# A 2-layer RG-LRU and HGRN2 step: the low parts of weight blocks made by an accumulating DMA onto a negated rounded block instead of a GpSimd subtraction

## The chip, the cores and the metric

The kernel runs on one core of one Trainium2 chip. A core has TensorE (PE in the profile: matrix products; PEld is its weight load), VectorE (DVE), ScalarE (ACT), GpSimd (POOL) and SyncE (SP), each with its own in-order instruction queue, and 16 DMA engines that move data between HBM and the on-chip memory SBUF. Products are collected in PSUM banks. The metric is the device time of one execution in microseconds, the median over runs.

## The reference

One inference step of a trunk with two layers, D = 1024, on 1024 prompt positions and on 8 sequences of 4 sampled positions (1056 columns in all). Layer 0 is an RG-LRU block, layer 1 is HGRN2 with 8 heads of 128; each is `x + y @ w_out`.

```python
def _lru_layer(x, g_norm, w_in, conv_w, conv_b, w_r, b_r, w_i, b_i, lam, w_out, h0, buf):
    xn = _rmsnorm(x, g_norm)
    u = xn @ w_in                                   # 1024 -> 2 * 1536
    xb, gate = u[..., :W_LRU], u[..., W_LRU:]
    xc, new_buf = _causal_conv(xb, conv_w, conv_b, buf)
    h, h_last = _rg_lru(xc, w_r, b_r, w_i, b_i, lam, h0)
    y = (h * jax.nn.silu(gate.astype(jnp.float32))).astype(x.dtype)
    return x + y @ w_out, h_last.astype(x.dtype), new_buf.astype(x.dtype)

def _hgrn_layer(x, g_norm, w_in, lb, o_gain, w_out, S0):
    xn = _rmsnorm(x, g_norm)
    u = (xn @ w_in).astype(jnp.float32)             # 1024 -> 4 * 1024
    q, f, iv, gate = jnp.split(u, 4, axis=-1)
    ...
    o, S_T = _hgrn2_chunked(q, k, v, log_g, S0)
    o = o * lax.rsqrt(jnp.mean(o * o, axis=-1, keepdims=True) + EPS) * o_gain.reshape(H_B, DV_B).astype(jnp.float32)
    y = (o.reshape(Bsz, T, INNER_B) * jax.nn.silu(gate)).astype(x.dtype)
    return x + y @ w_out, S_T.astype(x.dtype)
```

All data is float32.

## The kernel before

**Three products for one.** Each float32 operand is split into a high part, which is the operand rounded to the matmul's format fp32r, and a low part, which is what the rounding left over. A product is three matmuls (`mm3`, L242 to L244): high by high, high weight by low data, low weight by high data. So every weight block needs a `hi` and a `lo` tile before it can be used.

**Weights.** `weights()` (L365) loads a weight in blocks of 512 columns (128 x 512 floats are 256 KB; the output projection of layer 0 has blocks of 384, that of layer 1 has 512 + 128). For each block a DMA on SP's queue fills one of three raw buffers (`wraw`, L309), ScalarE rounds it into one of four `whi` buffers (L377), and `subtract` (L322) writes raw minus `whi` into one of four `wlo` buffers. The engine is the parameter `e`, GpSimd unless told otherwise; only four of the six weights at the very start use VectorE. Two of these weights at the start, numbers 3 and 5, are written into longer-lived tiles `yh` and `yl`, and the first two weights of the last projection into tiles called `t`. The raw buffer can be loaded again once both the rounding and the subtraction have read it; a `whi` or `wlo` buffer can be written again once the last matmul that used it is over.

**Where it is used.** Layer 0: gate and convolution projections (`project0`: one weight of two blocks, then three chunks of 352 columns with 8 x 3 matmuls each; `by_chunk` with two weights taken in turn), and the output projections `out`. Layer 1: the first two weights (`first1`), the two weights that follow them (`ahead`, L920) and the four weights of head 1. The last two weights of head 1 are taken in turn for the last chunks. Heads 2 to 7 use `seven` (L1398), a scheme of seven products for eight; its `split` (L1423) has a subtraction of its own on GpSimd, on the same line L322. The last projection (L1616) uses `weights()` again. The data's high and low parts `t` for `seven` come from VectorE, ScalarE and GpSimd (`t<-R,t` and `t<-tmp,t` on L322).

**Around the products.** While PE multiplies, the recurrence of the head before is worked out by short stages (`burst1` to `burst4`), with doubling multiplies on VectorE (L1033, L1042), small products on PE (L1051, L1105, L1136) and predicated copies (L1055). L1496 combines the products of `seven` on VectorE.

**What sets the order.** Nothing is issued where it stands in the code. A planner (`Flow`) records each operation with its engine, a cost, the tiles that it reads and writes and a priority; it then lays a list schedule forward and backward eight times, keeps the best, and issues the operations in that order. For layer 0 it also tries 3000 random changes within the first 60 us of its plan. In the plan a GpSimd operation over n columns costs 0.1 + 0.00245 n us, an ACT one 0.25 + 0.0007 n, a DMA's issue 0.45 plus a lag that grows with its size:

```python
        def dma(dst, src, r=(), w=(), prio=5, kb=180, q=Q):
            fl.add("SP" if q is Q else "ACT", 0.45, lambda: q.dma_start(dst, src), r, w, prio, kb * (1.0 if r else 0.75))
...
        return self.HOP + b[6] + (2.15 + a[5] / 250.0 if a[5] else 0.0)
```

A VectorE operation marked `both` is planned longer when GpSimd is busy. So a change of one operation's engine or cost can move others. At the start PE also gets 48 matmuls on a tile of ones (`warm`, L727), at the lowest priority.

Of the kernel before, what the change touches and what calls it, by code (L numbers as in the profile page):

```python
# [14 lines left out]
F32 = mybir.dt.float32  # L15
# [3 lines left out]
AF = mybir.ActivationFunctionType  # L19
ALU = mybir.AluOpType  # L20
# [190 lines left out]
def tile_trunk(ctx: ExitStack, tc: tile.TileContext, xT, prm, hc, w0, wg, wo0, w1, wo1, s_in,  # L211
               yT, h_out, c_out, sp_out, ss_out):
    nc = tc.nc
    V, S, G, T, Q = nc.vector, nc.scalar, nc.gpsimd, nc.tensor, nc.sync
# [80 lines left out]
    with ExitStack() as l0:  # L295
        pl = l0.enter_context(tc.tile_pool(name="l0", bufs=1, reuse_waits="tile"))
        fl = Flow("PE")
# [10 lines left out]
        def dma(dst, src, r=(), w=(), prio=5, kb=180, q=Q):  # L308
            fl.add("SP" if q is Q else "ACT", 0.45, lambda: q.dma_start(dst, src), r, w, prio, kb * (1.0 if r else 0.75))  # L309

        def act(n, emit, r, w, prio=5, more=0.0):
            fl.add("ACT", 0.25 + 0.0007 * n + more, emit, r, w, prio)

        def dve(n, emit, r, w, prio=5, both=False):
            fl.add("DVE", 0.13 + 0.0011 * n, emit, r, w, prio, both=both)

        def pool(n, emit, r, w, prio=5):
            fl.add("POOL", 0.1 + 0.00245 * n, emit, r, w, prio)

        def subtract(e, n, b, x, a, r, w, prio):  # L320

            emit = lambda: e.tensor_tensor(b, x, a.bitcast(F32), op=ALU.subtract)  # L322
            if e is G:
                pool(n, emit, r, w, prio)
            else:
                dve(n, emit, r, w, prio, True)
# [38 lines left out]
        def weights(src, n, prio=2, e=G, at=None, q=Q, own=()):  # L365

            own = iter(own)
            got = []
            for a in range(0, n, 512):
                m = min(512, n - a)  # L370
                raw, *rk = next(own, None) or next(raws)
                if at:
                    (hi, hk), (lo, lk) = ((o[:, a:a + m], k) for o, k in at)
                else:
                    (hi, hk), (lo, lk) = next(his), next(los)
                dma(raw[:, :m], src[:, a:a + m], (), rk, prio, m / 2, q)
                act(m, lambda hi=hi, raw=raw, m=m: S.copy(hi[:, :m], raw[:, :m]), rk, (hk,), prio)  # L377
                subtract(e, m, lo[:, :m], raw[:, :m], hi[:, :m], (*rk, hk), (lk,), prio)
                got.append((hi, lo, hk, lk))

            def get(k):
                q = slice((k % 4) * 128, (k % 4 + 1) * 128)
                hi, lo, hk, lk = got[k // 4]
                return hi[:, q], lo[:, q], (hk, lk)

            return get
# [18 lines left out]
        def project0(items):  # L405

            for src, evac in items:
                w = weights(src, 1024)
                for c in range(NCH):
                    evac(c, *product(w, xcols(c)))  # L410
                    yield

        def by_chunk(items):

            ws = [weights(src, 1024) for src, _ in items]
            for c in range(NCH):
                for w, (_, evac) in zip(ws, items):
                    evac(c, *product(w, xcols(c)))
                    yield


        def squares(k, x, xk, acc, eng=None, own=None, mult=False):

            a, ak = acc
            sq, sk = next(own or ts) if k else acc
            if mult:
                pool(CH, lambda: G.tensor_tensor(sq[:, :CH], x, x, op=ALU.mult), (xk,), (sk,), 2)
            else:
                act(CH, lambda: S.activation(sq[:, :CH], x, AF.Square), (xk,), (sk,), 2)
            if k:  # L430
                e = eng or G
                (pool if e is G else dve)(CH, lambda: e.tensor_tensor(a[:, :CH], a[:, :CH], sq, op=ALU.add), (sk, ak), (ak,), 2)
# [22 lines left out]
        def scaled_parts(c, k, x, xk, bc, bk, g, gk, e, prio=1):  # L455
            a, b = xh[k][:, chunk(c)], xl[k][:, chunk(c)]
            dve(CH, lambda: V.scalar_tensor_tensor(x, x, g, bc, op0=ALU.mult, op1=ALU.mult), (xk, bk, gk), (xk,), prio)
            act(CH, lambda: S.copy(a, x), (xk,), (("xh", k, c),), prio)
            subtract(e, CH, b, x, a, (xk, ("xh", k, c)), (("xl", k, c),), prio)
# [164 lines left out]
        def out(g, src, dst):  # L624

            own = cycle([next(xos) for _ in range(NXO)] + [next(ts) for _ in range(3)] + [(x[:, :CH], k) for x, k in (next(xbs) for _ in range(3))])
            for m in range(KD):
                w = weights(wo0[m][:, 384 * g:384 * g + 384], 384)
                for c in range(NCH):
                    ps, pk = product(w, ycols(c))  # L630
                    x, xk = next(own)
                    dma(x, src[m][:, chunk(c)], ((g, m, c),), (xk,), 3)
                    dve(CH, lambda x=x, ps=ps: V.tensor_tensor(x, ps[:, :CH], x, op=ALU.add), (pk, xk), (xk,), 0)
                    dma(dst[m][:, chunk(c)], x, (xk,), ((g + 1, m, c),), 3)
                    yield
# [207 lines left out]
        raw = (halves[1][:8], [slots[i] for i in (1, 4, 7, 2, 5, 8)] + [halves[1][8], free[8]], free[:8])  # L843
# [82 lines left out]
    with ExitStack() as l1:  # L926
        p1 = l1.enter_context(tc.tile_pool(name="l1", bufs=1, reuse_waits="tile"))
        fl = Flow(side=0.4)
# [704 lines left out]
        for m in range(KD):  # L1633
            row = (xh, xl)[m // 4][4 + m % 4]
            hi, lo, hk, lk = row[:, :nl], row[:, nl:2 * nl], ("late", m, 0), ("late", m, 1)
            for k in (hk, lk):
                inherit(k, [("x", p, m % 4, x) for p in (2, 3) for x in range(2)])
            raw, rk = next(raws)
# [60 lines left out]
        for a, n in OUT:  # L1699
# [4 lines left out]
            for m in range(KD):  # L1704
# [5 lines left out]
                hi, lo, wk = late[m]  # L1710
# [97 lines left out]
```

## Time and profile before

| | |
|---|---|
| time, 3 runs | 1086.44 us median (1086.31 to 1087.67) |
| span of the profiled execution | 1084.3 us |
| PE busy, share of the span | 1056.6 us, 97% |
| DVE / POOL / ACT busy | 885.3 / 602.3 / 549.2 us |
| bytes moved by DMA | 103.05 MB |

The profiled execution is one of the same program; its span runs from the first to the last instruction that the profiler saw, and its whole time is not given apart, so the runs' median stands 2.1 us above the span. In the profile's rows an instruction is written as engine, line, operation, output <- inputs, and the tile's size. The groups' `<-` in the last column names what ended the engine's idle time.

### The profile page before, as it was taken

To read this page: it belongs to the slowest core of one execution; us is meant where nothing else is said; L and a number is where in the kernel's file an instruction comes from. 1 tells how busy PE (TensorE), PEld (TensorE's weight loads), DVE (VectorE), ACT (ScalarE), POOL (GpSimd) and SP (SyncE) were. 2 spreads that over 40 slices of the span, in tenths; PEclk is the share of its full clock that TensorE was granted. 3 is DMA by queue.
4 is the path that set the end of the run, shared out by engine and by line. 5 is a ranking of instruction groups with operands and counts; after the bars stand their busy time and mean duration, and the time that the engine had idled before them with its cause. 6 is when DMAs were issued, how large, how long until landed. Compare 5 with 4: busy or idle time off the path is not lost.

```text
span 1084.3 us, 25492 instructions
## 1 busy us (share of the span) xinstructions
PE 1056.6 (97%) x9972; PEld 1027.9 (95%) x9972; DVE 885.3 (82%) x1661; ACT 549.2 (51%) x1249; POOL 602.3 (56%) x600
## 2 busy tenths in 40 slices
PE   9999999999999999999999999999999999999997
PEld 9999999999999999999899899999998989899996
DVE  8999995897996886275989999989989898995436
ACT  6578657868666964143433444443343434452323
POOL 3425453363452537356665876858686776752545
PEclk9999999999999999999999999999999999999998
DMA  9211222124822776240210121212121212355204
GB/s 299 60 26 42 56 55 66 55 67 133 279 83 66 223 251 180 95 134 30 60 41 24 48 92 43 99 44 89 39 77 51 89 42 67 111 179 164 77 7 160
DMA packets 70119, 103.05 MB, mean 95 GB/s; under 512 B 9200, under 2 KB 51184, under 8 KB 70000
## 3 DMA queue, kind: packets, MB, share of 16 engines
q1 hardware_dynamic: 67696, 98.67, 29.5%
q10 hardware_dynamic: 2304, 2.77, 0.7%
q8 instruction: 78, 1.28, 0.5%
q14 instruction: 41, 0.34, 0.1%
HBM read 71.05 MB, written 25.49 MB: 89 GB/s over the span
## 4 chain that ended last, share of the span: by engine, by line
PE 75%; DVE 20%; issue 3%; DMA 1%; POOL 0%; ACT 0%; POOLq 0%; ACTq 0%; DVEq 0%; SPq 0%
PE mm L242 21%; PE mm L243 20%; PE mm L244 20%; DVE k L1496 3%; DVE R L1033 2%; DVE sg L1042 2%; DVE sg L1033 2%; DVE R L1511 1%; PE hg L566 1%; DVE tmp L1365 1%; PE hg L1214 1%; PE hg L242 1%; PE hg L243 1%; PE hg L244 1%; PE hg L1268 1%
## 5 line engine op out<-in xcount | busy, mean ns | idle before, releaser
L242 PE MATMUL mm<-xh,whi 128*128 128x352 f32 (+1 forms) x1143 | 360.6, 315 | 1.7 <-DVE k L1496 1.6
L243 PE MATMUL mm<-xl,whi 128*128 128x352 f32 (+1 forms) x1143 | 354.4, 310 | 0.9 <-DVE xl L322 0.9
L244 PE MATMUL mm<-xh,wlo 128*128 128x352 f32 (+1 forms) x1143 | 354.2, 310 | 0.0
L322 POOL TENSOR_TENSOR wlo<-wraw,whi 128x512 fp32r<-128x512 f32 (+2 forms) x132 | 181.9, 1385 | 145.2 <-ACT whi L377 84.2
L242 PEld LDWEIGHTS mm<-xh,whi 128*128 128x128 f32 x1143 | 215.9, 189 | 4.4 <-DVE k L1496 2.5
L243 PEld LDWEIGHTS mm<-xl,whi 128*128 128x128 f32 x1143 | 216.2, 189 | 2.6 <-DVE xl L322 1.1
L244 PEld LDWEIGHTS mm<-xh,wlo 128*128 128x128 f32 x1143 | 216.0, 189 | 0.0
L498 DVE SCALAR_TENSOR_TENSOR k<-xb,prm_sb,k 128x352 f32<-128x352 f32 (+2 forms) x144 | 90.1, 637 | 10.9 <-ACT k L495 6.2
L242 PE MATMUL mm<-t,whi 128*128 128x264 f32 (+1 forms) x306 | 89.9, 294 | 7.1 <-DVE k L1496 7.1
L243 PE MATMUL mm<-t,whi 128*128 128x264 f32 (+1 forms) x306 | 87.7, 286 | 0.0
L244 PE MATMUL mm<-t,wlo 128*128 128x264 f32 (+1 forms) x306 | 87.6, 286 | 0.0
L581 POOL TENSOR_TENSOR k<-X 128x352 f32<-128x352 f32 x36 | 43.9, 1227 | 47.4 <-DVE R L582 37.8
L242 PEld LDWEIGHTS mm<-t,whi 128*128 128x128 f32 x306 | 57.6, 188 | 8.6 <-DVE k L1496 7.9
L1496 DVE TENSOR_TENSOR k<-mm,k 128x264 f32<-128x264 f32 x144 | 60.0, 425 | 5.2 <-issue 1.3
L322 POOL TENSOR_TENSOR wlo<-R,whi 128x512 fp32r<-128x512 f32 x32 | 46.1, 1442 | 28.1 <-ACT whi L1425 26.8
L377 ACT CAST whi<-wraw 128x512 fp32r<-128x512 f32 (+2 forms) x83 | 46.0, 574 | 29.9 <-PE mm L243 18.2
L244 PEld LDWEIGHTS mm<-t,wlo 128*128 128x128 f32 x306 | 57.6, 188 | 0.0
L243 PEld LDWEIGHTS mm<-t,whi 128*128 128x128 f32 x306 | 57.6, 188 | 0.0
L1033 DVE TENSOR_TENSOR R<-R,sg 128x512 f32<-128x512 f32 (+1 forms) x48 | 52.6, 1096 | 0.2
L242 PE MATMUL mm<-yh,whi 128*128 128x352 f32 x153 | 49.9, 326 | 0.0
L244 PE MATMUL mm<-yh,wlo 128*128 128x352 f32 x153 | 49.4, 323 | 0.0
L243 PE MATMUL mm<-yl,whi 128*128 128x352 f32 x153 | 49.4, 323 | 0.0
(479 smaller groups left out, 2714.8 us busy)
## 6 DMA issues: line engine op xcount, KB each, us to landing
wraw<-in_w_dram SPq DMA_DIRECT2D x90, 256.0 KB, 2.8
wraw<-in_wo_dram SPq DMA_DIRECT2D x34, 192.0 KB, 2.5
si<-in_s_in_dram SPq DMA_DIRECT2D x8, 512.0 KB, 4.6
out_ss_out_dram<-si SPq DMA_DIRECT2D x8, 512.0 KB, 2.6
R<-in_w_dram SPq DMA_DIRECT2D x15, 256.0 KB, 2.6
sg<-x1b SPq DMA_DIRECT2D x21, 176.0 KB, 2.9
x<-sg SPq DMA_DIRECT2D x21, 176.0 KB, 2.0
R<-td SPq DMA_DIRECT2D x72, 44.0 KB, 2.0
```

What stands on the lines that cost most here:

```text
L242: T.matmul(out, wh, xh, start=first, stop=False)
L243: T.matmul(out, wh, xl, start=False, stop=False)
L244: T.matmul(out, wl, xh, start=False, stop=last)
L322: emit = lambda: e.tensor_tensor(b, x, a.bitcast(F32), op=ALU.subtract)
L377: act(m, lambda hi=hi, raw=raw, m=m: S.copy(hi[:, :m], raw[:, :m]), rk, (hk,), prio)
L498: dve(u, lambda src=src, dst=dst, sh=sh, k=k: V.scalar_tensor_tensor(dst, sh(src, k), pc("cw", 12 * k + m), dst, op0=ALU.mult, op1=ALU.add ...
L566: fl.add("PE", 0.62, lambda ps=ps, i=i, c=c: T.matmul(ps[:96, :CH], gs[:, i, :], ST[:96, chunk(c)], start=True, stop=True), (("gs",), *((" ...
L581: pool(CH, lambda x=x, a=a, b=b: G.tensor_tensor(x, a.bitcast(F32), b.bitcast(F32), op=ALU.add), (ak, bk), (xk,), 3)
L1033: dve(n // 2, lambda sv=sv, dv=dv, s=s, f=f: V.tensor_tensor(dv[:, :, s, :], sv[:, :, s, :], f, op=ALU.mult), (*sk, *gk), dk if i == o els ...
L1042: dve(nb, lambda: V.tensor_tensor(g2, gv[:, :, 0], gv[:, :, 1], op=ALU.mult), gk, (k2,), 3, True)
L1214: T.matmul(ps[:, n * 128:(n + 1) * 128], kt[:, 4 * i + n, :], vt[:, 4 * i + n, :], start=True, stop=True)
L1496: dve(QT, lambda: V.tensor_tensor(o[0], z[0], u[0], op=ALU.add), (z[1], u[1]), (o[1],), 0)
```

## The change

In `weights()`, where the engine is GpSimd, the low part is no longer a subtraction. ScalarE, besides the rounding into `hi`, writes the negative of the block, rounded, into `lo`. Then a DMA issued from GpSimd's queue adds the raw block onto `lo` in SBUF (`accum_op=ALU.add`), which leaves raw minus rounded. The DMA reads the raw buffer, so that buffer is held until the DMA has landed. The four weights on VectorE and the subtractions of `seven` are as before. In the planner the DMA costs 1.0 us on GpSimd and has a lag by its size, like the loads.

```diff
+        def gather(dst, src, r, w, prio, kb):
+            fl.add("POOL", 1.0, lambda: G.dma_start(dst.bitcast(F32), src, accum_op=ALU.add), r, w, prio, kb)
+
         def act(n, emit, r, w, prio=5, more=0.0):
             fl.add("ACT", 0.25 + 0.0007 * n + more, emit, r, w, prio)
...
                 dma(raw[:, :m], src[:, a:a + m], (), rk, prio, m / 2, q)
                 act(m, lambda hi=hi, raw=raw, m=m: S.copy(hi[:, :m], raw[:, :m]), rk, (hk,), prio)
-                subtract(e, m, lo[:, :m], raw[:, :m], hi[:, :m], (*rk, hk), (lk,), prio)
+                if e is G:
+                    act(m, lambda lo=lo, raw=raw, m=m: S.activation(lo[:, :m], raw[:, :m], AF.Copy, scale=-1.0), rk, (lk,), prio)
+                    gather(lo[:, :m], raw[:, :m], (*rk, lk), (lk,), prio, m / 2)
+                else:
+                    subtract(e, m, lo[:, :m], raw[:, :m], hi[:, :m], (*rk, hk), (lk,), prio)
```

It touches 88 blocks: 58 of 128 x 512 and 16 of 128 x 384 and 6 of 128 x 128 through `wlo`, 4 `t` tiles and 4 `yl` tiles. Lines behind the edit have other numbers in the kernel after: L322 is L325, the rounding L377 is L380, the negated rounding is L382, the new DMA is L312, and what stood behind is 7 further on.

Since the planner sets the order, three places show what moved. The first is POOL in layer 1 while the recurrence of head 0 begins (`ab` is its small copy, `t_...` are data parts for `seven`, `wlo` a weight of head 1); before:

```order
L1092 COPY ab<-R 128x8x4
L322 TENSOR_TENSOR t_5208<-R,t_5207 128x264
L322 TENSOR_TENSOR t_5206<-R,t_5205 128x264
L322 TENSOR_TENSOR t_5210<-tmp,t_5209 128x264
L322 TENSOR_TENSOR t_5206<-R,t_5205 128x264
L322 TENSOR_TENSOR wlo<-wraw,whi 128x512 x2
L322 TENSOR_TENSOR t_5208<-R,t_5207 128x264
L322 TENSOR_TENSOR t_5210<-R,t_5209 128x264 x2
```

and in the kernel after, at the same place:

```order
L1099 COPY ab<-R 128x8x4
L325 TENSOR_TENSOR t_5274<-tmp,t_5273 128x264
L325 TENSOR_TENSOR t_5272<-R,t_5271 128x264
L325 TENSOR_TENSOR t_5270<-R,t_5269 128x264 x2
L312 DMA wlo<-wraw 128x512 x2
L325 TENSOR_TENSOR t_5272<-R,t_5271 128x264
L325 TENSOR_TENSOR t_5274<-R,t_5273 128x264 x2
L325 TENSOR_TENSOR t_5272<-R,t_5271 128x264
```

Two DMA issues stand where two subtractions stood; POOL's data parts around them are the same but for one pair's order. The second place is ACT at the weights of head 1's later items (`sg` and `k` are evacuations of products, `R` and `a` belong to the recurrence); before:

```order
L1001 COPY sg<-mm 128x320
L1368 COPY t_5205<-R 128x264
L991 COPY vrep<-mm 128x96
L377 COPY whi<-wraw 128x512 x2
L1368 COPY t_5207<-R 128x264
L1368 COPY t_5209<-R 128x264
L1036 COPY R<-R 128x64x8
L1006 ACTIVATE k<-mm 128x352
```

and after:

```order
L1008 COPY sg<-mm 128x320
L382 ACTIVATE wlo<-wraw 128x512
L998 COPY vrep<-mm 128x96
L382 ACTIVATE wlo<-wraw 128x512
L1375 COPY t_5271<-R 128x264
L1043 COPY R<-R 128x64x8
L1043 COPY a<-sg 128x64x8
L380 COPY whi<-wraw 128x512 x2
```

The negated roundings come first and the plain roundings behind the recurrence's copies. The third is PE at the start of the program; before:

```order
L727 MATMUL hg<-ones 128x128 x29
L242 MATMUL mm<-xh,whi 128x352
L243 MATMUL mm<-xl,whi 128x352
L244 MATMUL mm<-xh,wlo 128x352
L242 MATMUL mm<-xh,whi 128x352
L243 MATMUL mm<-xl,whi 128x352
L244 MATMUL mm<-xh,wlo 128x352
L727 MATMUL hg<-ones 128x128 x9
```

and after:

```order
L734 MATMUL hg<-ones 128x128 x48
L242 MATMUL mm<-xh,whi 128x352
L243 MATMUL mm<-xl,whi 128x352
L244 MATMUL mm<-xh,wlo 128x352
L242 MATMUL mm<-xh,whi 128x352
```

The 48 matmuls on ones now all stand ahead of the first product; before, 19 of them stood between the first products.

## The prediction

> **What bounds the kernel now.** I read the page's head first, then the table of stretches, then TensorE's (PE's) list of waits, and last the timeline of each place where PE stands still.
>
> ```profile
> span 1084.3 us, 25492 instructions
> PE 1056.6 (97%) x9972; PEld 1027.9 (95%) x9972; DVE 885.3 (82%) x1661; ACT 549.2 (51%) x1249; POOL 602.3 (56%) x600
> ```
>
> PE is busy for 1056.6 of 1084.3 us. The change leaves its matmuls alone, so all it can win lies in the 27.7 us in which PE is idle, and in what a lowered clock costs. The stretches say where that is (columns: stretch, PE busy, weight loads, VectorE = DVE, ScalarE = ACT, GpSimd = POOL, granted clock, DMA share, GB/s).
>
> ```profile
> 0.00:40.00 40.00, 37.84 (x253) 37.03 (x254) 34.28 (x77) 26.86 (x56) 18.35 (x23) 1.00 0.71 231
> ...
> 360.00:400.00 40.00, 40.00 (x247) 39.27 (x246) 31.73 (x48) 30.84 (x51) 21.99 (x15) 1.00 0.84 254
> 400.00:520.00 120.00, 120.00 (x751) 119.36 (x751) 70.91 (x136) 44.14 (x97) 67.14 (x72) 1.00 0.36 112
> 520.00:540.00 20.00, 19.48 (x301) 18.63 (x299) 19.76 (x35) 9.39 (x23) 13.57 (x14) 1.00 0.10 28
> 540.00:545.00 5.00, 1.54 (x129) 1.42 (x129) 4.96 (x7) 1.60 (x3) 3.53 (x3) 0.90 0.36 108
> 545.00:550.00 5.00, 5.00 (x24) 5.00 (x25) 4.94 (x11) 1.55 (x3) 1.29 (x1) 0.76 0.02 5
> ...
> 600.00:640.00 40.00, 37.01 (x441) 35.29 (x440) 39.02 (x68) 17.03 (x52) 31.91 (x27) 0.96 0.25 81
> ...
> 940.00:950.00 10.00, 7.03 (x53) 6.42 (x53) 9.13 (x19) 4.61 (x13) 3.22 (x3) 1.00 0.45 134
> ```
>
> In the body of layer 0 (360 to 520) PE has no gap: a faster POOL can win nothing there, it can only lose. Around 520 to 550, 600 to 640 and 940 to 950 DVE is full and PE is not: those stretches end with DVE. PE's list of waits agrees (what it waited for: us in total, times, longest).
>
> ```profile
> PE mm L242 <- DVE k L1496: 8.7, 9, 1.5
> PE hg L1051 <- DVE sg L1033: 5.3, 5, 2.3
> PE hg L1105 <- DVE a L1033: 1.6, 1, 1.6
> ...
> PE mm L243 <- DVE xl L322: 0.9, 1, 0.9
> ```
>
> No entry names POOL or a low part `wlo`. So the weights' subtraction is never what PE waits for; it can matter only through what it does to DVE. The timelines of POOL, DVE and PE at the worst place (start, duration, instruction, in brackets the idle time before it) show that it does something.
>
> ```profile
> 538.06 3.16 POOL L322 TENSOR_TENSOR wlo<-wraw,whi 128x512 fp32r<-128x512 f32 x2
> 541.18 2.35 POOL L322 TENSOR_TENSOR t<-R,t 128x264 fp32r<-128x264 f32 x2
> ...
> 525.80 1.17 DVE L1033 TENSOR_TENSOR R<-R,ST 128x528 f32<-128x528 f32 x1
> 528.07 1.80 DVE L1033 TENSOR_TENSOR R<-R,sg 128x528 f32<-128x528 f32 x1
> ...
> 538.32 1.77 DVE L1033 TENSOR_TENSOR R<-R,sg 128x512 f32<-128x512 f32 x1
> 540.01 1.75 DVE L1033 TENSOR_TENSOR sg<-sg 128x512 f32<-128x512 f32 x1
> ...
> 546.52 0.69 DVE L1033 TENSOR_TENSOR a<-a,sg 128x512 f32<-128x512 f32 x1
> ...
> 541.82 0.76 PE L1051 MATMUL hg<-R,sg 128*32 128x32 f32 x64 [2.34 <-DVE sg L1033]
> 544.22 0.73 PE L1105 MATMUL hg<-R,a 128*16 128x16 f32 x64 [1.64 <-DVE a L1033]
> ```
>
> The same DVE multiply takes 0.69 us with POOL idle and 1.77 and 1.75 us beside the two `wlo` subtractions, and PE's two gaps (2.34 and 1.64 us) end with such multiplies. The Trainium skill has a rule for it (SBUF — State Buffer, "Who interferes with whom"): a DVE instruction with two SBUF inputs contends with a GpSimd instruction that reads SBUF, and not with one that only writes it. The rows agree with its first half; no run here yet shows the second, which by that page speaks for the change.
>
> **The change part by part.** 88 weight blocks lose their POOL subtraction; each gains an ACT pass (raw block times -1, rounded) and an accumulating DMA from POOL's queue that adds the raw block onto it. The 84 subtractions of the heads 2 to 7 stay.
>
> ```profile
> L322 POOL TENSOR_TENSOR wlo<-wraw,whi 128x512 fp32r<-128x512 f32 (+2 forms) x132 | 181.9, 1385 | 145.2 <-ACT whi L377 84.2
> ...
> L377 ACT CAST whi<-wraw 128x512 fp32r<-128x512 f32 (+2 forms) x83 | 46.0, 574 | 29.9 <-PE mm L243 18.2
> ```
>
> POOL loses about 88 x 1.39 = 122 us of work, ACT gains about 88 x 0.57 = 50 us. Neither total is on the path: ACT goes from 51% to some 56%, and in its fullest stretch above (360 to 400) it has 9 us of 40 free. That hides ACT's pass; without that cover each would cost its 0.57 us.
>
> *A, the stall at 538 to 550.* What leaves DVE when no subtraction runs beside it: 1.77 - 0.69 = 1.08, 1.75 - 0.69 = 1.06, 1.80 - 0.69 = 1.11 and 1.17 - 0.69 = 0.48, together 3.7 us. DVE is full here, so PE's gaps (2.34 + 1.64 = 4.0) can shrink by as much as DVE comes earlier. After the gaps the clock falls: in 545 to 550 only 24 matmuls fit into 5 us, while 751 in 120 us is 0.16 us each, so 24 would take 3.84; that is 1.2 us more to win if the gap closes wholly. Best case -5.0 (both gaps and most of the clock loss), worst 0 (issuing the DMA holds DVE up as the subtraction did). I take **-3.7**: POOL's two `t` subtractions at 541.18 stay, so some stretch stays.
>
> *B, 600 to 640.* PE idles 40 - 37.01 = 3.0 us behind a full DVE. No `wlo` of a changed block lies inside, so only the lead that DVE brings along can help. Head 1's last blocks give such a lead:
>
> ```profile
> 557.54 1.73 POOL L322 TENSOR_TENSOR wlo<-wraw,whi 128x512 fp32r<-128x512 f32 x1
> ...
> 558.05 1.52 DVE L1365 TENSOR_TENSOR R<-R,xh 128x264 f32<-128x264 f32 x1
> 559.60 0.43 DVE L1365 TENSOR_TENSOR R<-R,xl 128x264 f32<-128x264 f32 x1
> ```
>
> That is 1.1 us there. Some will be lost in waits for PE's own products: **-1.0**, between -3.0 and 0.
>
> *C, 940 to 950*, where the output projection's first weights are made:
>
> ```profile
> 945.04 1.56 POOL L1192 TENSOR_TENSOR vb<-vst,bm 96x512 fp32r<-96x512 f32 x1 [5.10 <-DMA ST<-x]
> 946.56 1.70 POOL L322 TENSOR_TENSOR t<-wraw,t 128x128 fp32r<-128x128 f32 x2
> ...
> 946.08 2.75 DVE L1033 TENSOR_TENSOR sg<-a,sg 128x528 f32<-128x528 f32 x1
> ...
> 949.56 0.39 PE L242 MATMUL mm<-t,whi 128*128 128x264 f32 x1 [1.54 <-DVE k L1496]
> ```
>
> A 0.7 us multiply takes 2.75 us, and PE then idles 1.54 us for DVE. The two `t` subtractions go, `vb` stays (0.5 us of the overlap): 2.75 - 0.7 - 0.5 = 1.5. I take **-1.5**, between -1.5 and 0.
>
> *D, the low part becomes ready later.* This is the price. Until now it follows the cast by one POOL instruction; from now on it needs ACT's pass (0.6), the issue on POOL and the landing. Before shows no DMA of POOL's and no accumulate. The nearest rows for the landing (source, engine, count, KB, us from issue to landing):
>
> ```profile
> wraw<-in_w_dram SPq DMA_DIRECT2D x90, 256.0 KB, 2.8
> ...
> ST<-k SPq DMA_DIRECT2D x36, 44.0 KB, 1.8
> ...
> wraw<-in_w_dram ACTq DMA_DIRECT2D x2, 256.0 KB, 5.2
> ```
>
> Landing: from 1.8 (44 KB inside SBUF) to 5.2 (256 KB in the crowded start). It is nearest to the 2.8 of a load of the same size, with something for reading the destination as well: 3.2. Issue: no less than nothing, no more than the 1.3 us of a POOL instruction on the tile; I take 1.0. Together 4.2, between 1.8 and 6.5. How much room is there? Within a stage a block's buffers are free for a whole item of 72 matmuls, 72 x 0.16 = 11.5 us, before they are read, which hides it. The tight places are three changes of stage: layer 0's last weights to layer 1's first, the fourth weight of layer 0's gate where it goes chunk by chunk, and head 1's last two items, which are taken in turn. At the first, ACT's casts show when buffers come free:
>
> ```profile
> 504.03 0.62 ACT L377 CAST whi<-wraw 128x512 fp32r<-128x512 f32 x1 [0.85 <-PE mm L243]
> 505.93 0.62 ACT L377 CAST whi<-wraw 128x512 fp32r<-128x512 f32 x1 [1.29 <-PE mm L243]
> ...
> 506.63 1.29 POOL L322 TENSOR_TENSOR wlo<-wraw,whi 128x512 fp32r<-128x512 f32 x1 [0.59 <-ACT whi L377]
> ```
>
> The block that comes free at 504.03 is read again after 36 matmuls, at about 509.8: 5.8 us, less ACT's 0.6 and a hop leaves 4.9 for issue and landing. 4.2 fits. Queued behind the gather on POOL are ST's and a's gates, which PE does not need for another product. So **+0.5** (part of one miss), between 0 and 3 x (6.5 - 4.9) = +4.8.
>
> *E, traffic.* Each gather moves 256 KB more. In 360 to 400 the DMA engines are 84% busy at 254 GB/s; 256 KB takes 1.0 us at that rate. Four blocks fall there; the 11.5 us of room hide that, if not it is +4. I take **+0.5**.
>
> *F, the start.* All 48 warm-up matmuls now stand ahead of the first product, before only 29; PE's work to 40 us is the same. Two low parts go through the DMA and stand behind a power on POOL. The matching PE waits of before are near 1 us each: **0**, between -2 and +2.
>
> The sum: -3.7 - 1.0 - 1.5 + 0.5 + 0.5 + 0 = -5.2 on the span of 1084.3. The median of the runs is 1086.4, so 2.1 us lie around the span; 1079.1 + 2.1 = 1081.2, about **1081 us**.
>
> **The rivals.**
>
> *R1, issuing holds DVE as the subtraction did.* POOL works through the block's addresses for about as long as it now subtracts. For: the `vb` multiply, which is no subtraction, stretches DVE at 946.08 too. Against: an address list is small beside the 512 columns that a subtraction reads. A, B and C are then nil, D and E stay at +1.0: 1087.
>
> *R2, the low part lands late: slower.* The one mechanism is the time from ACT's pass to the landing at the three tight places. It decides from 4.9 us on. DVE is full between 520 and 560; if it holds POOL's issue up as POOL holds DVE up, the issue costs 1.8 us (the longest stretched pair), and landing as in the crowded start 5.2: 7.0, which is 2.1 too late, three times, 6.3, and 2 at the start. PE then waits for `wlo`, where now it never does. Half of the 6.2 of A to C is still won, 0.5 of E is paid: -3.1 + 6.3 + 2.0 + 0.5 = +5.7, 1092. For: the rows for DMAs reach it. Against: they reach it only when many loads start at once. The skill's same page tells in its trap "DVE blocks DMA" of a DMA from GpSimd that took some 3.1 us instead of 0.62 beside a DVE copy; that would be 2.5 us per block and speaks for R2. No row of before can show it.
>
> *R3, traffic in 360 to 400 costs its whole +4* and eats the gain: -6.2 + 0.5 + 4 = -1.7, 1084.7. Against: PE has no gap there, so no load is late yet.
>
> *R4, more is won*: A and B at their best, C too, D and E hidden: -5.0 - 3.0 - 1.5 = -9.5, 1077.
>
> **How the numbers follow.** Chances: forecast 0.42, R1 0.16, R2 0.27, R3 0.08, R4 0.07. A measurement of this kernel can tell 0.2%, 2.2 us, from no change, so faster is below 1084.2. The forecast's own range is 1078 to 1084.5. Faster: nearly all of the forecast and R4, 0.48; same: most of R1, R3 and a little of the forecast, 0.21; slower: R2 and the rest of R1, 0.31. The range goes from R4's 1077 to 1094, 2 us beyond R2's 1092, since about half of R2 lies above its own figure.
>
> **What would show it.** A: DVE's L1033 multiplies of head 0 at 0.7 us and the waits of L1051 and L1105 on DVE shorter by 3 to 4 us in all; if they stay, R1. D: PE's list of waits names no DMA onto `wlo`; if it does, with more than 2 us in all, R2, and the issues' landing tells whether 4.9 was passed. E: PE at 40.00 in 360 to 400. The forecast is wrong if POOL's issue takes longer than the 1.4 us that it replaces, or the landing passes 4 us.

## The result, and the profile after

The kernel after takes 1081.36 us (median of 4 runs, 1078.10 to 1081.68), the kernel before 1086.88 us on the same chip: a ratio of 0.9943, 95% interval 0.9929 to 0.9957, so 5.5 us less. The profiled execution of the kernel after was the 1078.10 one, with a span of 1076.3 us. A second profiled execution of it, among the experiments, had a span of 1079.6 us and is the more usual one. Both are used below.

First the head of the page, the row of the new DMA (source, queue, count, KB, us from issue to landing), and the groups of the issue and of ScalarE's negated pass.

```profile
span 1076.3 us, 25689 instructions
PE 1055.4 (98%) x9972; PEld 1027.1 (95%) x9972; DVE 829.9 (77%) x1661; ACT 589.3 (55%) x1337; POOL 556.8 (52%) x600
...
L312 POOL DMA_DIRECT2D wlo<-wraw x80 | 70.8, 928 | 134.5 <-ACT wlo L382 117.8
...
L382 ACT ACTIVATE wlo<-wraw 128x512 fp32r<-128x512 f32 (+1 forms) x80 | 45.5, 583 | 35.0 <-PE mm L244 26.2
...
wlo<-wraw POOLq DMA_DIRECT2D x58, 256.0 KB, 4.0
```

An issue costs POOL 0.93 us where the subtraction cost 1.39, and the low part lands 4.0 us after the issue. ACT has 40 us more, POOL 46 us less. The largest change is one that nothing in the diff names: VectorE (DVE) is busy 55 us less (885.3 to 829.9) with the same 1661 instructions. The stretches (same columns as before):

```profile
360.00:400.00 40.00, 39.41 (x241) 38.39 (x240) 25.31 (x43) 33.98 (x52) 13.21 (x14) 1.00 0.95 267
...
520.00:540.00 20.00, 20.00 (x305) 19.37 (x304) 19.62 (x38) 11.32 (x27) 11.95 (x16) 1.00 0.36 97
540.00:545.00 5.00, 5.00 (x152) 4.75 (x152) 4.96 (x10) 2.68 (x6) 2.32 (x4) 1.00 0.83 180
545.00:550.00 5.00, 5.00 (x33) 5.00 (x32) 4.86 (x11) 1.71 (x3) 1.15 (x1) 1.00 0.11 36
...
600.00:640.00 40.00, 37.36 (x514) 35.28 (x513) 36.37 (x70) 18.41 (x55) 30.80 (x26) 1.00 0.25 90
...
940.00:950.00 10.00, 10.00 (x211) 9.46 (x211) 8.58 (x23) 4.93 (x15) 5.90 (x8) 1.00 0.82 185
```

Between 520 and 550 and between 940 and 950 PE has no gap any more, and its clock stays at 1.00 where it had fallen to 0.76. At 360 to 400, where it had none, it now has 0.6 us. PE's list of waits names what that is:

```profile
PE mm L242 <- DVE k L1503: 5.4, 5, 1.5
PE hg L1058 <- DVE sg L1040: 2.9, 4, 0.8
...
PE mm L244 <- DMA wlo<-wraw: 0.6, 1, 0.6
```

The waits on the combining line (L1496, now L1503) went from 8.7 to 5.4 us, those of L1051 (now L1058) from 5.3 to 2.9, L1105's 1.6 is gone, and one wait for a landing is new.

**Where the time went, read by marks.** PE's order in layer 1 is the same in both kernels but for a few small products, so the same instruction can be found in each trace, and its start compared. One such mark, before and after (the first matmuls of head 0's third stage):

```profile
553.98 0.46 PE L1129 MATMUL mm<-R,a 128*32 128x32 f32 x32
```

```profile
551.42 0.46 PE L1136 MATMUL mm<-R,a 128*32 128x32 f32 x32
```

So there the kernel after is 2.56 us ahead. The same subtraction at eight marks, for all kernels of this study (us against the profiled execution of before; negative is ahead; the columns are the mark's start in the kernel before):

| kernel | 521 | 554 | 611 | 653 | 700 | 936 | 951 | 1053 |
|---|---|---|---|---|---|---|---|---|
| after | 2.7 | -2.6 | -2.6 | -5.0 | -4.4 | -5.0 | -8.8 | -8.3 |
| after, second execution | 4.6 | -0.8 | -0.8 | -1.6 | -1.7 | -1.8 | -5.5 | -5.0 |
| e1_layer1 | 0.4 | -4.7 | -4.8 | -5.6 | -5.6 | -5.9 | -8.7 | -8.7 |
| e2_layer0 | 3.2 | 0.8 | 0.9 | 1.0 | 1.0 | 1.1 | 1.1 | 1.5 |
| e3_pool_add | 6.2 | 6.6 | 9.7 | 8.6 | 8.6 | 8.1 | 4.6 | 5.1 |
| e4_split_too | 4.7 | -0.7 | 1.2 | -4.1 | -6.2 | -15.1 | -18.8 | -17.9 |
| e5_layer1_split | -0.1 | -5.5 | -4.0 | -9.3 | -11.3 | -20.1 | -23.9 | -23.6 |
| e6_no_start | 12.9 | 7.7 | 8.0 | 7.2 | 7.3 | 7.0 | 4.2 | 4.7 |
| e7_heads | -0.3 | -5.6 | -5.4 | -6.4 | -7.4 | -15.9 | -15.8 | -15.6 |
| e8_last | 0.2 | 0.6 | 0.6 | 0.6 | 0.4 | 0.2 | -3.6 | -3.4 |
| e9_split_pool_add | -0.2 | -5.5 | -5.0 | -4.7 | -6.7 | -6.8 | -10.3 | -9.7 |
| e10_before_order | 0.3 | -4.4 | -4.4 | -3.8 | -3.9 | -3.6 | -6.0 | 0.1 |

The first row is the result in short: layer 0 loses 2.7 us (4.6 in the second execution), the stall at 540 gives 5.3 (5.4), the part to 653 gives 2.4 (0.8), the heads 3 to 7 nothing, the last projection's start 3.8 (3.7), and the end takes 0.5 back. The two executions differ by 1.9 us in layer 0 and by another 1.6 us between 611 and 653. There the granted clock stayed at 1.00 in the profiled execution (the row 600 to 640 above), while it fell in the second one, as it does in the kernel before (0.96 in both); the second execution's row is:

```profile
600.00:640.00 40.00, 37.38 (x466) 35.40 (x469) 35.98 (x67) 17.02 (x52) 31.35 (x26) 0.96 0.26 87
```

These two places explain why the profiled execution was faster than the others.

### The profile page after: what moved, and what is told of

Same layout as the page of the kernel before. It is cut to its first block, busy times and chain, and to the rows that moved or that the text cites. A ratio compares the mean times of both kernels' runs of the same rounds, so it can differ in the third digit from the quotient of the medians.

```text
span 1076.3 us, 25689 instructions
## 1 busy us (share of the span) xinstructions
PE 1055.4 (98%) x9972; PEld 1027.1 (95%) x9972; DVE 829.9 (77%) x1661; ACT 589.3 (55%) x1337; POOL 556.8 (52%) x600
## 4 chain that ended last, share of the span: by engine, by line
PE 82%; DVE 14%; issue 2%; DMA 1%; POOL 0%; ACT 0%; SPq 0%; POOLq 0%; DVEq 0%; ACTq 0%
PE mm L242 22%; PE mm L243 22%; PE mm L244 22%; DVE k L1503 2%; DVE sg L1040 2%; DVE R L1040 2%; DVE sg L1049 2%; PE hg L573 1%; PE hg L734 1%; DVE R L1518 1%; PE hg L1275 1%; PE hg L1221 1%; PE hg L1058 1%; PE hg L242 1%; PE hg L243 1%
## 5 line engine op out<-in xcount | busy, mean ns | idle before, releaser
L242 PE MATMUL mm<-xh,whi 128*128 128x352 f32 (+1 forms) x1143 | 357.0, 312 | 1.1 <-ACT xh L1375 1.0
L312 POOL DMA_DIRECT2D wlo<-wraw x80 | 70.8, 928 | 134.5 <-ACT wlo L382 117.8
L325 POOL TENSOR_TENSOR wlo<-wraw,whi 128x512 fp32r<-128x512 f32 x52 | 72.7, 1400 | 37.4 <-ACT whi L1432 36.9
L505 DVE SCALAR_TENSOR_TENSOR k<-xb,prm_sb,k 128x352 f32<-128x352 f32 (+2 forms) x144 | 77.4, 545 | 17.9 <-ACT k L502 8.9
L1503 DVE TENSOR_TENSOR k<-mm,k 128x264 f32<-128x264 f32 x144 | 60.0, 426 | 8.4 <-PE mm L244 5.1
L382 ACT ACTIVATE wlo<-wraw 128x512 fp32r<-128x512 f32 (+1 forms) x80 | 45.5, 583 | 35.0 <-PE mm L244 26.2
L325 POOL TENSOR_TENSOR wlo<-R,whi 128x512 fp32r<-128x512 f32 x32 | 46.3, 1448 | 28.6 <-ACT whi L1432 28.6
```

What stands on the lines that cost most here:

```text
L242: T.matmul(out, wh, xh, start=first, stop=False)
L312: fl.add("POOL", 1.0, lambda: G.dma_start(dst.bitcast(F32), src, accum_op=ALU.add), r, w, prio, kb)
L382: act(m, lambda lo=lo, raw=raw, m=m: S.activation(lo[:, :m], raw[:, :m], AF.Copy, scale=-1.0), rk, (lk,), prio)
L505: dve(u, lambda src=src, dst=dst, sh=sh, k=k: V.scalar_tensor_tensor(dst, sh(src, k), pc("cw", 12 * k + m), dst, op0=ALU.mult, op1=ALU.add ...
L1503: dve(QT, lambda: V.tensor_tensor(o[0], z[0], u[0], op=ALU.add), (z[1], u[1]), (o[1],), 0)
```

## The experiments

The theory was that POOL's subtraction stretches the DVE multiplies beside it and that the DMA does not; the rival, that the planner's other order did it. All ratios are to the kernel before on the same chip.

**e1_layer1 and e2_layer0: which layer.** The gather only in one of the two plans. (`fl.side` tells them apart.)

```diff
-                if e is G:
+                if e is G and fl.side < 1:
```

> The gather only in layer 1; in layer 0's plan (with layer 1's first four weights) the subtraction as in the kernel before. My theory: the gain is DVE's relief at 538 to 550, 600 to 640 and 940 to 950, all in layer 1, and layer 0 lost 2.7 us in the profile of the kernel after (start, one wait of 0.6 us for a landing at 399, a slightly slower pace). So about 1081.4 - 2.7 = 1078.7 us; L1051's and L1105's waits at 540 (2.3 and 1.6 us) are gone, PE has no gap for a low part in layer 0. Rival (the gain comes from the planner's other order as such, layer 0's included): no better than 1081, waits anywhere.

> The gather only in layer 0's plan; layer 1 as in the kernel before. My theory: nothing to win there, so the time of before plus the 2.7 us, about 1089.6 us; the waits of 2.3 and 1.6 us at 540 and of 1.5 us at 950 are back. Rival (layer 0's lag in the profile is drift between executions): 1086.9, as before.

Measured: e1_layer1 1076.62 us, ratio 0.9892 (0.9865 to 0.9918), against 1081.4 of the kernel after; e2_layer0 (`fl.side > 1`) 1091.33 us, ratio 1.0035 (1.0021 to 1.0049), slower than before. So the whole gain is in layer 1 and layer 0's edit is a loss of some 4 us. In e2_layer0 the waits at 540 and at 950 are back. The row of e2_layer0 shows something else: of its lag of 3.2 us at 521 only 0.8 is left at 554. DVE is the bound there, and when PE comes later, PE waits less. A lag of layer 0 is partly swallowed by the stall behind it, but not once that stall is gone.

**e3_pool_add: the order of the kernel after, with POOL reading again.** The one line of `gather`:

```diff
-            fl.add("POOL", 1.0, lambda: G.dma_start(dst.bitcast(F32), src, accum_op=ALU.add), r, w, prio, kb)
+            fl.add("POOL", 1.0, lambda: G.tensor_tensor(dst, src, dst.bitcast(F32), op=ALU.add), r, w, prio, kb)
```

> The order of the kernel after on every engine, with ACT's negated pass, but POOL adds the raw block itself with a tensor_tensor that reads both from SBUF, in place of issuing a DMA. My theory (contention of POOL's reads with DVE's): the L1040 multiplies beside it take 1.7 us again, PE's gaps near 540 and 945 come back, 5.3 + 3.8 us at most, and layer 0's loss goes: 1081.4 + 9.1 - 2.7 = 1088, at least 1085. Rival (the other order, or the low part no longer waiting for the cast, is what helped): about 1081.

Measured: 1090.60 us, ratio 1.0028 (1.0016 to 1.0039). The timelines of the same place in the two kernels show why; the order of all engines is the same but for one DVE instruction at 145 us, and only the POOL instruction differs. The kernel after, POOL and DVE (start, duration):

```profile
538.58 1.78 POOL L312 DMA_DIRECT2D wlo<-wraw  x2 [0.28 <-PE hg L1058]
539.83 1.31 POOL L325 TENSOR_TENSOR t<-R,t 128x264 fp32r<-128x264 f32 x1
...
538.51 0.68 DVE L1040 TENSOR_TENSOR R<-R,sg 128x512 f32<-128x512 f32 x1
539.11 0.68 DVE L1040 TENSOR_TENSOR sg<-sg 128x512 f32<-128x512 f32 x1
539.72 1.99 DVE L1040 TENSOR_TENSOR R<-R,sg 128x512 f32<-128x512 f32 x1
```

and e3_pool_add, POOL, DVE and PE:

```profile
543.91 3.15 POOL L312 TENSOR_TENSOR wlo<-wraw,wlo 128x512 fp32r<-128x512 f32 x2
...
544.16 1.77 DVE L1040 TENSOR_TENSOR R<-R,sg 128x512 f32<-128x512 f32 x1
545.86 1.75 DVE L1040 TENSOR_TENSOR sg<-sg 128x512 f32<-128x512 f32 x1
...
547.66 0.76 PE L1058 MATMUL hg<-R,sg 128*32 128x32 f32 x64 [1.92 <-DVE sg L1040]
549.52 0.68 PE L1112 MATMUL hg<-R,a 128*16 128x16 f32 x59 [1.09 <-DVE a L1040]
```

Beside two issues the multiplies take 0.68 us, beside two additions that read SBUF 1.77 and 1.75, as beside the subtractions before. And the third multiply of the kernel after, beside `t<-R,t`, which still reads SBUF, takes 1.99. So the order alone gains nothing at 540 (6.2 to 6.6 in the table), and the contention theory holds there. But it doesn't hold at 940: e3_pool_add goes from 8.1 to 4.6, a gain of 3.5 us with POOL reading as much as before. And its layer 0 lags by 6.2 us without a single accumulating DMA; 4.5 us of this are lost by 60 us, behind two waits of 1.73 us for DVE and a fall of the granted clock right behind the second (0.54 in 40 to 42), where the kernel after has lost 0.8 (1.4 in the second execution). Both are against what I had expected of this run.

**e8_last and e7_heads: the last projection alone, and the heads 0 and 1 alone.** Conditions `fl.side < 1 and n < 1024` and `fl.side < 1 and n == 1024`.

> The gather only for the last projection's weights. If the gain at 940 to 950 is made there: 1086.9 - 3.3 = 1083.6 us, with the waits of 2.3 and 1.6 us at 540 as before and none of 1.5 us at 950. Rival (it needs the lead from 540): 1087.

> The gather in layer 1 only for weights of 1024 columns (heads 0 and 1), the last projection as before, in the order of before there. If the gain at 940 to 950 belongs to the last projection's own blocks and their place in the order, PE's waits of 1.1 and 1.5 us on L1503 are back there: 1076.6 + 3 = 1079.6 us, and the waits at 540 stay away. Rival (that gain is VectorE's lead from 540 carried on): 1076.6.

Measured: e8_last 1083.81 us, ratio 0.9965 (0.9951 to 0.9979). It gains 3.8 us from 936 to 951 and nothing elsewhere: that gain is made there and needs no lead from 540. e7_heads 1070.77 us, ratio 0.9854 (0.9834 to 0.9873), 6 us better than with the last projection's gathers as well, which neither theory had. Its waits at 940 are back (1.15 and 1.56 us), as its first guess had it; but by the table its heads 3 to 7 gain 8.5 us between 700 and 936, although POOL subtracts there exactly as before. Its timeline shows the same POOL work at another phase. Before, DVE and POOL in head 3:

```profile
709.92 3.25 DVE L1033 TENSOR_TENSOR sg<-a,sg 128x528 f32<-128x528 f32 x1
...
708.59 1.50 POOL L1192 TENSOR_TENSOR vb<-vst,bm 96x512 fp32r<-96x512 f32 x1
710.06 1.28 POOL L322 TENSOR_TENSOR wlo<-R,whi 128x512 fp32r<-128x512 f32 x1
711.31 1.29 POOL L1433 TENSOR_TENSOR wraw<-R,wraw 128x512 f32<-128x512 f32 x1
```

and in e7_heads:

```profile
701.84 0.75 DVE L1040 TENSOR_TENSOR sg<-a,sg 128x528 f32<-128x528 f32 x1
...
700.51 1.50 POOL L1199 TENSOR_TENSOR vb<-vst,bm 96x512 fp32r<-96x512 f32 x1
702.18 1.55 POOL L325 TENSOR_TENSOR wlo<-R,whi 128x512 fp32r<-128x512 f32 x1 [0.17 <-ACT whi L1432]
```

Before, the multiply that PE waits for starts inside POOL's work and is held for 3.25 us; here it starts at the end of `vb`, with a pause of 0.17 us behind it, takes 0.75, and the later collisions hit DVE instructions that nobody waits for. The order decides *which* DVE instruction collides. In the heads 3 to 7 the order of e7_heads differs from that of before by two operations a head, which stand earlier (L1518 on DVE and L1513 on POOL), and the heads begin in another phase; whether it is these operations or the phase was not tried apart.

**e4_split_too: the weights' subtractions in `seven` by DMA as well.** POOL still makes low parts of data (`t`, `xl`) by subtraction. In `split` of `seven`:

```diff
-                subtract(G, 512, lo, raw, hi, (rk, hk), (lk,), 2)
+                act(512, lambda: S.activation(lo, raw, AF.Copy, scale=-1.0), (rk,), (lk,), 2)
+                gather(lo, raw, (rk, lk), (lk,), 2, 256)
```

> The kernel after, and the 84 subtractions of the heads 2 to 7 (split of seven) are made by ACT's negated pass and the gather as well. If POOL's reads stretch DVE there too, the heads' waits (L242 on the combining L1503, five of 1.1 to 1.5 us, and L1058 on L1040, five of 0.75) shrink by about half, -5 us: 1076.5. Rival (those waits are DVE's own work, not stretched): within 1 us of 1081.4. Second rival: the landing of some 4 us is too late for the products of seven, which then wait for wlo: slower than 1083.

Measured: 1067.86 us, ratio 0.9816 (0.9792 to 0.9840), more than twice the gain that I expected at best. The second rival shows on a small scale: at the start of the heads with `seven` PE waits once for a landing, and e5_layer1_split has the same wait (1.47 us).

```profile
604.74 0.39 PE L244 MATMUL mm<-t,wlo 128*128 128x264 f32 x1 [1.45 <-DMA wlo<-wraw]
```

**e5_layer1_split: the two that won, together.** e1_layer1 and e4_split_too.

> The gather in layer 1 alone, and there in the split of seven too: the two edits that won put together. If they add, layer 0's loss (4.3 us when layer 0 alone had the gather) comes off the 1067.9 us of the kernel with all gathers: about 1064 us; PE's waits on L1503 and L1058 in the heads 3 to 7 are absent. Rival (VectorE, full at 520 to 640, absorbs layer 0's lag anyway): 1067 to 1068.

Measured: 1064.17 us (1062.96 to 1065.58), ratio 0.9788 (0.9769 to 0.9808). They add. This is the fastest kernel of the study, 2.1% below the kernel before.

**e9_split_pool_add: is it the order or the reads in the heads?** e5_layer1_split with the splits' gathers done by a POOL addition, in the same order.

```diff
-                gather(lo, raw, (rk, lk), (lk,), 2, 256)
+                fl.add("POOL", 1.0, lambda: G.tensor_tensor(lo, raw, lo.bitcast(F32), op=ALU.add), (rk, lk), (lk,), 2, 256)
```

> The kernel with the gather in layer 1 and in the split of seven (1064.2 us), in its order on every engine, but the splits of the heads 2 to 7 add the raw block on POOL with a tensor_tensor that reads SBUF, in place of the DMA. If the 2.5 us that each head gained come from POOL's reads being gone: they come back, PE waits on L1503 (about 1.3 us) and L1058 (about 0.75) in each head, 1064 + 6 x 2.5 = 1079 us. Rival (the other order does it, as in the kernel with head 0's and 1's gathers alone, whose heads 3 to 7 also ran without those waits though POOL subtracts there): 1064 to 1067.

Measured: 1076.16 us, ratio 0.9892 (0.9873 to 0.9911). The stretch of the heads 3 to 7 (columns as above) in the kernel before, the kernel after, e5_layer1_split, e9_split_pool_add and e7_heads, one row each in this order:

```profile
660.00:900.00 240.00, 231.67 (x3244) 222.72 (x3244) 220.02 (x414) 100.19 (x274) 168.76 (x149) 1.00 0.20 65
```

```profile
660.00:900.00 240.00, 231.88 (x3250) 223.07 (x3249) 218.94 (x412) 98.85 (x271) 169.68 (x150) 1.00 0.19 66
```

```profile
660.00:900.00 240.00, 240.00 (x3477) 231.45 (x3478) 179.88 (x426) 133.57 (x345) 146.49 (x155) 1.00 0.59 133
```

```profile
660.00:900.00 240.00, 233.67 (x3267) 224.58 (x3265) 195.06 (x403) 128.83 (x340) 179.07 (x151) 1.00 0.20 68
```

```profile
660.00:900.00 240.00, 240.00 (x3445) 231.68 (x3444) 205.22 (x426) 106.08 (x293) 185.78 (x155) 1.00 0.20 67
```

PE idles 8.3, 8.1, 0, 6.3 and 0 us. With e5's order, POOL's reads bring the waits back; the first entry of PE's list of waits in e9_split_pool_add (the combining line is L1504 there):

```profile
PE mm L242 <- DVE k L1504: 8.1, 7, 1.7
```

In that order the DMA decides. With e7's order POOL may read and PE has no gap. Over the whole kernel, in the same order, DVE is busy 850.4 us in e9_split_pool_add and 806.6 us in e5_layer1_split: 44 us more for the same 1661 instructions.

**e10_before_order: the gather in the order of before.** Layer 1's gathers, but planned like the subtraction that they replace (its cost, behind the cast, no lag; the negated pass at no cost), so that PE, DVE and POOL keep before's order but for a few rows in the last projection.

```diff
-                    gather(lo[:, :m], raw[:, :m], (*rk, lk), (lk,), prio, m / 2)
+                    fl.add("POOL", 0.1 + 0.00245 * m, lambda lo=lo, raw=raw, m=m: G.dma_start(lo[:, :m].bitcast(F32), raw[:, :m], accum_op=ALU.add), (*rk, hk, lk), (lk,), prio)
```

> The gather in layer 1 alone, but planned as the subtraction was (same cost, after the cast, no lag), so that PE, VectorE and POOL keep the order of the kernel before up to the last 150 us. Contention theory for 540: PE's waits of 2.3 and 1.6 us there go, about -5 us by 554. Order theory for 940 to 950: its two waits of 1.1 and 1.5 us on L1503 stay, and 600 to 640 and the heads stay as before: 1086.9 - 5 = 1082 us. If contention also made the gain at 940 to 950: 1078.

Measured: 1086.77 us, ratio 0.9988 (0.9978 to 0.9997): nearly all of the gain is lost, at a place that neither theory had. PE's gaps and one cast of ACT in its timeline, and its stretch from 950 to 955:

```profile
541.07 0.69 PE L1112 MATMUL hg<-R,a 128*16 128x16 f32 x64 [0.60 <-DVE a L1040]
...
939.92 0.39 PE L242 MATMUL mm<-xh,whi 128*128 128x264 f32 x1 [0.38 <-DVE k L1503]
941.97 0.36 PE L242 MATMUL mm<-t,whi 128*128 128x264 f32 x1 [0.33 <-DVE k L1503]
953.91 0.43 PE L242 MATMUL mm<-xh,t 128*128 128x352 f32 x1 [1.43 <-ACT xh L1589]
...
953.38 0.48 ACT L1589 CAST xh<-k 128x352 fp32r<-128x352 f32 x1 [2.11 <-DMA k<-yd]
...
950.00:955.00 5.00, 3.44 (x25) 2.89 (x23) 2.27 (x6) 2.41 (x7) 2.52 (x4) 1.00 1.01 275
```

The stall at 540 goes (0.3 to -4.4) without any change of order: there contention is enough. From 936 to 951 the gain is 2.4 us, with the two waits of 1.1 and 1.5 us shrunk to 0.4 and nothing. So at 940 either the DMA in the old order (2.4) or the new order with POOL reading (3.5) removes most of the stall; I had expected order alone. Nothing is won between 554 and 653, so what the kernel after has there belongs to its order (0.8 us), or to the clock that did not fall in its profiled execution (the other 1.6 us of the 2.4). And then 6 us are lost from 951 on: the DMA engines are full (1.01), an ACT cast waits 2.11 us for data that is still on its way, PE 1.43 us for the cast. Right behind this gap the granted clock falls (0.78, 0.50 and 0.87 in the three stretches of 2 us from 955 on), and at 974.87 PE waits 0.83 us more, for POOL's `xl`. I read this as the price of a plan that does not know the transfers' lag and puts them on top of other loads; ACT's unplanned passes may have a part in it, which was not tried apart.

**e6_no_start: is layer 0's loss made at the start?** The gather everywhere but for the four `yl` blocks (`fl.side < 1 or not at`).

> The kernel after, but the two weights at the very start (4 blocks, yl) are subtracted on POOL as before. If layer 0's loss is made at the start (VectorE's xl is waited for at 18 to 45 us), it goes: 1081.4 - 3 = 1078.4 us. Rival (it is the landing that PE waits for at 399 and a slower pace under more DMA traffic): no better than 1080.5.

Measured: 1089.89 us, ratio 1.0017 (1.0004 to 1.0030), 8.5 us slower than the kernel after. The first guess fell. The rival's bound, no better than 1080.5, holds, and the wait for a landing in layer 0 has grown from 0.6 to 2.62 us; but a loss of this size was in neither guess. Two of PE's gaps in its layer 0:

```profile
35.90 0.66 PE L242 MATMUL mm<-xh,yh 128*128 128x352 f32 x1 [2.83 <-DVE sg L533]
...
407.13 0.43 PE L244 MATMUL mm<-xh,wlo 128*128 128x352 f32 x1 [2.62 <-DMA wlo<-wraw]
```

Behind each gap the granted clock falls (0.50 in 36 to 38 and in 408 to 410). With fewer DMAs the plan of layer 0 comes out worse, by 12.9 us at 521 against 2.7 to 4.7 for the plan of the kernel after. So what layer 0 loses depends on the order that the planner's search happens to find, and not on the number of gathers alone.

**e11_after_again: the kernel after once more.**

> The kernel after once more. Its profiled execution took 1078.1 us, the three others 1081.2 to 1081.7. If that is the start of layer 0, where two other kernels with the same layer 0 showed 0.3 to 2 us more of waits: about 1081.4 us, with a lag behind the kernel before of 2.6 to 4.7 us at the end of layer 0. If the kernel after has two ways to run: some executions near 1078 again.

Measured: 1080.96 us (1079.01 to 1081.35), ratio 0.9932 (0.9917 to 0.9947); its lag at 521 is 4.6 us, within the expected 2.6 to 4.7. Its one wait for a landing, in PE's timeline:

```profile
400.90 0.43 PE L244 MATMUL mm<-xh,wlo 128*128 128x352 f32 x1 [1.04 <-DMA wlo<-wraw]
```

So of the 3.3 us between the two profiled executions 1.9 us lie in layer 0 and about 1.5 us in the fall of the clock at 628 to 632, which the first one did not have. One of the runs here took 1079.01 us, so executions near 1078 do come again, as the second guess had it; why some escape these losses was not found.

## Why the prediction was right, point by point

The predicted 1081 us and the sign were right, and the likeliest case was the one that came. Its sum was right because errors of both signs met: the gains were larger than put, and so was layer 0's loss. In the second execution A and C give 3.9 us more than put and layer 0 costs 3.6 us more. That these cancel is luck. R4 had put A to C at 9.5 us together; they came to 9.9 us, and 11.5 in the profiled execution, and only layer 0 kept the total at the forecast.

**A, the stall at 540: right in mechanism, too small.** I took -3.7 us from the four multiplies' relief, with -5.0 as the best case. Measured -5.3 and -5.4: the gaps close wholly, so the lowered clock (0.76) goes as well, which I had kept out of the value that I took. e3_pool_add (new order, reads: no gain) and e10_before_order (old order, no reads: 4.7) show that it is POOL's reads and not the order. One row was misread: the multiply of 0.69 us at 546.52 does not have POOL idle, for a `t` starts at 546.53. The multiply just ahead of it does, and took the same time, so the sum stands:

```profile
545.92 0.69 DVE L1033 TENSOR_TENSOR R<-R,sg 128x512 f32<-128x512 f32 x1
```

R1, that issuing would hold DVE as the subtraction did, is refuted by 0.68 us beside the issue. The Trainium skill (SBUF — State Buffer, "Who interferes with whom") has this as the half of its rule that no row of before could show: a GpSimd instruction that only writes SBUF does not contend with a DVE instruction with two SBUF inputs. The multiplies beside the issues, 0.68 us, agree with it, if an issue is such an instruction, which no run shows by itself.

**B, 600 to 640: right in size, wrong in cause.** Put at -1.0, measured -2.4 and -0.8 up to 653; 1.6 us of the -2.4 are the clock that did not fall. I took it as DVE's lead carried on. e10_before_order has that lead and gains nothing there; e3_pool_add has none and gains 1.1 from 611 to 653. So the rest of it is the order. (Before that, at 579, e3_pool_add loses 3.1 us behind two waits of 1.43 and 1.34 us that no other kernel shows.)

**C, 940 to 950: the term that failed in size.** Put at -1.5 with that as the best case, since `vb` stays; measured -3.8 and -3.7. I had priced one stretched multiply, and one gap of 1.54, but the planner also moved POOL's copy `gp`, the `t` blocks and `vb` against DVE's work, so that all gaps of that stretch (3.0 us) went. In the kernel after, the multiply that took 2.75 us takes 0.70, beside issues:

```profile
938.37 1.74 POOL L312 DMA_DIRECT2D t<-wraw  x2 [3.99 <-ACT t L380]
...
938.99 0.70 DVE L1040 TENSOR_TENSOR sg<-a,sg 128x528 f32<-128x528 f32 x1
```

e3_pool_add gains 3.5 there from the order alone, e10_before_order 2.4 from the DMA alone. The two overlap; they are not two shares of a sum.

**D, the landing: right in the median.** Issue and landing were put at 1.0 and 3.2 us, with room of 4.9 for both. Measured 0.93 for the issue, and 4.0 (4.2 in the second execution) from the start of the issue to the landing, so for both together, inside the room. Single landings took up to 7.5 us. PE waits for a landing once, 0.6 and 1.0 us, at 399, in the stage of layer 0's gate that goes chunk by chunk; +0.5 was taken. R2 did not come: the longest issue took 1.2 us, at 528, with DVE full. R3 did not come either: 360 to 400 cost PE 0.6 us and not 4. The 3.1 us that R2 took from the Trainium skill stand on the page SBUF — State Buffer under "A bandwidth-pool intuition that's wrong", for a whole DMA beside a DVE copy, not for its issue. Beside the issues of this kernel DVE ran no plain copy from SBUF to SBUF, so that case was not tried here.

**E and F, layer 0: put at +0.5 and 0, measured with D +2.7 and +4.6.** This is the step that was mis-sized. I looked for the loss in traffic and in the start's weights. More marks split it (us against before, at marks of before):

| kernel | 60 | 360 | 400 | 521 |
|---|---|---|---|---|
| after | 0.8 | 1.6 | 2.6 | 2.7 |
| after, second execution | 1.4 | 3.0 | 4.4 | 4.6 |
| e3_pool_add | 4.5 | 5.9 | 6.0 | 6.2 |
| e1_layer1 | 0.4 | 0.4 | 0.4 | 0.4 |

The start costs 0.8 to 1.4 us, where F was put at 0. From 360 to 400 another 1.0 to 1.4 us are lost, of which the wait for the landing is 0.6 to 1.0; e3_pool_add, without the DMA, loses 0.1 there, so this part is the gather's. The rest is a pace that is slightly lower all along, 0.8 to 1.6 us from 60 to 360. e3_pool_add has that too (1.4), so it is not the transfers; e1_layer1, with the order of before and the subtraction, has none. Whether the other order or ACT's added pass slows it stays open, since no run has the gather in layer 0 in the order of before.

**What should have shown it.** L1033's multiplies at 0.7 us: yes beside the issues, 1.99 beside `t`. L1051's and L1105's waits shorter by 3 to 4 us: together 6.9 before, 3.6 after (2.9, and 0.7 of one on another bank). PE at 40.00 in 360 to 400: no, 39.41. A DMA onto `wlo` in PE's list: yes, 0.6 and 1.0 us, less than the 2 us that would have meant R2. The last sign, a landing past 4 us, was set too low: 4.0 and 4.2 us came, and the forecast held.

**What I left out altogether** was that the 84 subtractions that stay have the same price. The heads 3 to 7 had 8.3 us of PE's idle time in the profile before, behind the same stretched multiplies (3.25 us at 709.92). That was worth more than anything in the change, as e5_layer1_split shows.

## What to carry to other kernels

Before asking what an engine off the critical path costs, look for the instructions of the full engine that take two or three times their usual duration, and for who runs beside them: here two POOL subtractions that nobody waited for, 3.2 us together, held up the multiplies behind which PE stood still for 2.3 us. Moving such work to a DMA paid in layer 1, where DVE was full; in layer 0, where PE had no gap, it lost some 4 us. So do it by stage, and let the plan know the transfer's lag. Where a planner sets the order, run a control with the new order and the old instruction, and one with the old order and the new instruction: a gain at a collision can come from either.

## What the runs showed of the hardware that was not expected

A DMA issue on POOL took 0.86 to 1.2 us and left DVE multiplies of 512 columns at 0.68 us, while POOL additions of two SBUF operands held them to 1.75 and 1.77. In the same order DVE is busy 829.9 us with the issues and 873.2 us with the additions (e3_pool_add), 43 us for 88 blocks, and 44 us for 84 blocks between e5_layer1_split and e9_split_pool_add: in both pairs a POOL instruction that reads costs DVE 0.5 us on average. The accumulating DMA of 256 KB inside SBUF landed 4.0 us after its issue in the median, against 2.9 for a load of the same size from HBM in the same execution (4.2 and 3.0 in the second execution).
